# Hybrid decoder layer on one core: q, k and x transposed on TensorE in place of DMA transposes

## The chip, the cores and the metric

The kernel runs on one core of one Trainium2 chip. The metric is the device time of one execution in microseconds; the median of three runs counts. Engines are named as the profile names them: PE is TensorE, PEld its weight loads, DVE is VectorE, ACT is ScalarE, POOL is GpSimd, SP is the engine whose queue issues most DMAs.

## What is computed

One layer of a decoder (2048 positions, 1024 channels): an RMS norm, one input projection, three causal mixers side by side, and one output projection.

```
h = rms_norm(x, norm_g);  proj = h @ w_in
FoX (8 heads of 64):   softmax(q.k/8 + c[t] - c[s], s <= t) @ v,   q and k RMS-normed, c = cumsum(log_sigmoid(ff + b_f))
pooling (4 groups):    (trailing mean over 2/4/8/16 positions - the token) @ w_pool * scale
stick-breaking (4 heads): a = exp(log_sigmoid(z) + sum of -softplus(z) after s), s < t;  a @ v
out = x + concat(fox * silu(g), pool * silu(g), stick * silu(g)) @ w_out
```

Inputs and output are float32. The kernel keeps that precision by splitting each operand of a large matmul into a float16 high part and a float16 low part.

## The kernel before

**Stages.** Positions are cut into 16 blocks of 128 rows. Stage a is the projection and attention of FoX heads 0 to 3, stage b of heads 4 to 7, stage s of the four stick-breaking heads with the pooling projection (p) between its blocks, and stage o the output projection. In the profiled execution they lie roughly at 0 to 470, 470 to 820, 820 to 1235 and 1235 to 1416 us; they overlap at the edges. Sequence order is reversed, so block i attends to blocks 0 to i.

**A block's input.** `transpose_rows` (line 371) takes 128 rows of x, writes high and low parts side by side into a tile `pp` of 128x2048 f16 (`pairs16`, lines 341 and 342: one ACT cast, one DVE subtraction), and one DMA transpose turns it into `xT` (`xTx` in the trace), with channels on the partitions. `project` (line 315) then runs 24 matmuls of 128x512 per 512 output columns (`pqk`, `pvg`). Stage a makes x this way; the transposed x is also parked in DRAM (`keep_x`) and stages b, s and p load it from there (`xTb`, `xTs`, `xTp`). Stage o makes its own (`xTm` from `ppm`).

**q and k.** `stacks` (line 455) writes high and low parts of q and k of a block into `st` (128x1024 f16, by two calls of `pairs16`), and one DMA transpose on SP's queue turns it into `qT`. Five projection segments later `place` (line 466) runs on DVE: one copy puts k into the column block of `Kc` (line 467), two copies of 64x512 swap q's halves inside `qT` (line 469). Each of the 48 blocks of stages a, b and s does this once.

**Attention.** For each head `scores` (line 396) takes a PSUM tile `sp` of 128x1024 f32. The tag `sp` has two such tiles, two banks each. In stages a and b DVE reads it (line 736), in stage s ACT does (the sigmoid, line 875). ACT takes the exponential (line 746) or DVE scans (line 883), ACT or DVE casts the high part, POOL subtracts for the low part (`split_t`, lines 430 to 433), and a DMA transpose on SP's queue turns the weights into `tt` (line 435) for `pv`.

**What sets the order.** `projections` is a stream of segments of three matmuls (`SEG`: 16 per block), and the loop at the end advances it between heads by a table of goals (`LEADS`, `DEPTH`). `later(k, fn)` postpones work by k segments. From that program order a scheduler derives each engine's order; every engine then works its own list strictly from the front, with semaphores between them.

Of the kernel before, what the change touches and what calls it, by code (L numbers as in the profile page):

```python
# [10 lines left out]
F16 = mybir.dt.float16  # L11
# [7 lines left out]
P = 128  # L19
KT = 8  # L20
# [10 lines left out]
LB = 4  # L31
SPD = 6
KPD = 2
MXD = 0
GTD = 0
BAL = 1
GR4 = 0
GR2 = 1
QSB = 2
SWE = 'vv'  # L40
KCE = 'v'
SCD = 5
M5 = 2
FE = 's'
OMS = 'g'
# [72 lines left out]
KB = 5  # L118
QB = 1
QNB = 1  # L120
QTB = 3
WINDOWS = (2, 4, 8, 16)


# [1 line left out]
def hybrid(ctx: ExitStack, tc, xN, w_in, w_pT, w_out, ng, b_f, qg, kg, w_pool, p_scale, bands, out):  # L126
# [19 lines left out]
    def pick(pattern, k):  # L146
        return {"v": v, "g": g, "s": s}[pattern[k % len(pattern)]]
# [223 lines left out]
    def transpose_rows(src, scale, tag, park=None):  # L371
        pp = at.tile([P, 2 * D], F16, name=f"pp{tag}", tag="pp", bufs=PB)
        pairs16(pp[:, 0:D], pp[:, D:2 * D], src, scale[:, 0:1], pick(XLO, park or 0))
        x = xp.tile([P, 2, KT, P], F16, name=f"xT{tag}", tag="xT", bufs=XB)
        sy.dma_start_transpose(x.rearrange("p a k t -> p (a k) t"), pp)
        if park is not None:
            keep_x(park, x)
        return x

    def keep_x(j, x):  # L380
        later(KPD, lambda: dq(QPARK).dma_start(xTd[j], x))
# [68 lines left out]
    def heads(ap):  # L450
        return ap.rearrange("p (h d) -> p h d", h=NH)

    placed, spread_, mixed = set(), set(), set()

    def stacks(tag, j, qsrc, ksrc, sc, Kc):

        st = at.tile([P, 2, NH, P], F16, name=f"st{tag}", tag="qs", bufs=QSB)
        pairs16(st[:, 0, :, 0:HD], st[:, 0, :, HD:P], heads(ksrc), sc)
        pairs16(st[:, 1, :, 0:HD], st[:, 1, :, HD:P], heads(qsrc), sc)
        qT = at.tile([P, 2 * NH, P], F16, name=f"qT{tag}", tag="qT", bufs=QTB)  # L460
        if j % 4 == 3:
            Kc[j // 4] = big.tile([P, NH, 512], F16, name=f"K{tag}", tag="K", bufs=KB)
        o_ = (j % 4) * P
        sy.dma_start_transpose(qT, st.rearrange("p a h d -> p (a h d)"))

        def place():
            pick(KCE, 0).tensor_copy(Kc[j // 4][:, :, o_:o_ + P], qT[:, 0:NH])
            for k in range(2):
                pick(SWE, k).tensor_copy(qT[k * HD:k * HD + HD, 0:NH], qT[HD - k * HD:P - k * HD, NH:2 * NH])  # L469
            placed.add(tag)  # L470

        later(SCD, place)
        return qT

    def values(ph, i, j, Vc, src):
        if i % 4 == 0:
# [17 lines left out]
    class Fox:  # L494
        def __init__(self, ph, w, cols):
            self.ph, self.w, self.cols = ph, w, cols
            self.first = ph == "a"
            self.col = 0 if self.first else 256
            self.Vc = {}
            self.ctx = {}  # L500
            self.late = []

        def start(self):
# [200 lines left out]
        def stages(self, i, j, pqk):  # L704
            ph = self.ph
            qn = at.tile([P, 512], F32, name=f"qn{ph}_{i}", tag="qn", bufs=QNB)
            s.activation(qn, pqk, AF.Square)
            ss = sm.tile([P, 8], F32, name=f"ss{ph}_{i}", tag="ss")
            yield
            v.tensor_reduce(ss, qn.rearrange("p (h d) -> p h d", d=HD), AX.X, ALU.add)  # L710
            v.tensor_scalar(ss, ss, self.i2[:, 0:1], EPS, ALU.mult, ALU.add)
            f = sm.tile([P, 8], F32, name=f"f{ph}_{i}", tag="f")
            rsqrt(f, ss, 8, f"qk{ph}_{i}")
            yield
            v.tensor_scalar(f, f, self.iq[:, 0:1], None, ALU.mult, ALU.bypass)
            v.tensor_tensor(qn.rearrange("p (h d) -> p h d", d=HD), pqk.rearrange("p (h d) -> p h d", d=HD),
                            f.unsqueeze(2).broadcast_to([P, 2 * NH, HD]), ALU.mult)
            g.tensor_tensor(heads(qn[:, 256:512]), heads(qn[:, 256:512]), gain.unsqueeze(1).broadcast_to([P, NH, HD]), ALU.mult)
            yield
            self.ctx[i] = stacks(f"{ph}_{i}", j, qn[:, 0:256], qn[:, 256:512], 1.0, self.Kc)  # L720

        def qk(self, i, h):
            ph, negc = self.ph, self.negc
            j = NT - 1 - i
            qT = self.ctx[i]
            cs = list(chunks(j * P))
            n_ = len(cs)
# [59 lines left out]
    class Stick(Fox):  # L787
        def __init__(self, w):
            self.ph, self.w = "s", w
            self.Vc, self.ctx, self.late = {}, {}, []  # L790
            self.first = False
            self.col = 768
            self.vr, self.own = {}, {}
# [48 lines left out]
        def proj(self, i, x):  # L842
            w = self.w
            j = NT - 1 - i
            pqk = pj.tile([P, 512], F32, name=f"pqks_{i}", tag="pj")
            if i in IS:
                pvg = pj.tile([P, 512], F32, name=f"pvgs_{i}", tag="pj")
                yield from together([project(pqk, x, w, 0, 0, 512), project(pvg, x, w, 0, 512, 512)])
            else:
                yield from project(pqk, x, w, 0, 0, 512)  # L850
            qT = stacks(f"s_{i}", j, pqk[:, 0:256], pqk[:, 256:512], 1.0 / WS, self.Kc)
            if i not in IS:
                pvg = pj.tile([P, 512], F32, name=f"pvgs_{i}", tag="pj")
                yield from project(pvg, x, w, 0, 512, 512)
            vt = at.tile([P, NH, P], F16, name=f"vr_{i}", tag="fq", bufs=2)
            pairs16(vt[:, :, 0:HD], vt[:, :, HD:P], heads(pvg[:, 0:256]), 1.0 / WS)
            self.vr[i] = vt
            keep_gate("s", i, j, pvg[:, 256:512], w.iw, 768)
            self.steps(i, j)
            self.ctx[i] = qT  # L860

        def qk(self, i, h):
            j = NT - 1 - i
            qT = self.ctx[i]
            parts = []
            rprev = None
            if h == 0:
# [252 lines left out]
    def projections():  # L1120
        for u, (n, i) in enumerate(units):
            need_x(u + (2 if units[u + 2:u + 3] == [(4, 0)] and OA else LAH[n]))
            if i == 0 and n:
                phases[n].start()
            gen = phases[n].proj(i, xs.pop(u, None))
            yield from with_tail(gen) if (n, i) == (4, 0) else gen
            if i == NT - 1 and n < 3:
                with first(HLW):
                    load_weights((1, 2, 4)[n])
            if n == 2 and i == 1:  # L1130
                load_weights(3)
# [84 lines left out]
    with tc.manual_schedule(engines={mybir.EngineType.PE}) if MAN else nullcontext():  # L1216
        opening()
        for k, (n, i) in enumerate(plan):
# [2 lines left out]
            advance(base)  # L1221
            for h in range(NH):
                key = f"{ph.ph}_{i}"
                if key not in placed or ph.ph != "s" and key not in spread_:
                    tick(1 << 30)
                assert key in placed and (ph.ph == "s" or key in spread_)
                with first(HAT):
                    pending.append((ph, i, h, *ph.qk(i, h)))
                advance(base + (goal[k] - base) * (h + 1) // NH)
                drain(DEPTH)  # L1230
            ph.ctx.pop(i)
            if n == 1 and M5 <= i < M5 + 4:
                for kt in range(2 * (i - M5), 2 * (i - M5) + 2):
                    phases[3].fold(kt)
# [78 lines left out]
```

## Time and profile before

| | us |
|---|---|
| median of three runs (1412.66 to 1419.62) | 1414.28 |
| profiled execution | 1417.73 |
| its span, first to last instruction | 1415.7 |

| engine | busy share of the span |
|---|---|
| PE | 85% |
| DVE | 70% |
| ACT | 50% |
| POOL | 45% |
| 16 DMA engines, the SP/ACT queue with the transposes | 80.4% |

A busy share is a mean over four stages with different limits. PE's busy time counts from the start of a matmul to its modelled end, so two that overlap are not added. "issue" in a chain of waits is time in which an engine waited for nothing that the profile shows.

### The profile page before, as it was taken

The page shows a single profiled execution, that of the slowest core. Times are in us where ns is not written, and L with a number is a line of the kernel's source. Part 1 is how long each engine was busy: PE and PEld are TensorE (multiplying, and loading weights), DVE is VectorE, ACT ScalarE, POOL GpSimd, SP SyncE. Part 2 cuts the span into 40 slices and gives each one's busy share as a digit, 9 for nine tenths or more (in the row PEclk, how much of TensorE's full clock was granted, in tenths as well). Part 3 has the DMA queues.
Part 4 walks back from the last instruction along what each step waited for, and adds up shares of the span by engine and source line. Part 5 has one row for each costly group of instructions (what it writes and reads, how often), then busy time and mean ns, then how long its engine had stood idle before and what let it go on. Part 6 is the DMA issues. An engine that isn't in the chain of part 4 may idle for free.

```text
span 1415.7 us, 24981 instructions
## 1 busy us (share of the span) xinstructions
PE 1209.6 (85%) x9068; PEld 642.2 (45%) x9068; DVE 997.1 (70%) x2093; ACT 702.0 (50%) x1356; POOL 634.1 (45%) x615
## 2 busy tenths in 40 slices
PE   7788879787887889897987888978988997779998
PEld 3344445444444445454544544444544553444443
DVE  5777889889998567786888655556574669865731
ACT  6555546555554446664667644545455564432210
POOL 0133345445455234553656654555455464623300
PEclk9889899999998989999999999999999999989999
DMA  6689999998999999996999998687886888999853
GB/s 215 176 169 203 214 188 221 200 196 182 210 210 209 210 227 207 202 177 135 184 217 191 227 207 186 146 158 161 173 175 142 172 196 226 225 277 287 225 160 89
DMA packets 617068, 275.25 MB, mean 194 GB/s; under 512 B 552561, under 2 KB 590833, under 8 KB 616945
## 3 DMA queue, kind: packets, MB, share of 16 engines
q1 hardware_dynamic: 605600, 239.93, 80.4%
q10 hardware_dynamic: 10832, 33.67, 7.9%
q8 instruction: 71, 1.16, 0.4%
q14 instruction: 53, 0.43, 0.1%
q0 software_dynamic: 512, 0.07, 0.0%
HBM read 102.60 MB, written 34.67 MB: 97 GB/s over the span
## 4 chain that ended last, share of the span: by engine, by line
PE 18%; DVE 11%; issue 9%; DMA 8%; POOL 8%; ACT 5%; SPq 1%; POOLq 0%; ACTq 0%; DVEq 0%
PE pr L319 11%; DVE rrs L883 5%; POOL pps L433 5%; DMA qTs<-sts 2%; DMA qTb<-stb 2%; PE pqks L319 2%; DVE Lb L736 2%; DMA xTm<-ppm 1%; ACT pps L430 1%; ACT Lb L746 1%; POOL rrs L877 1%; PE sps L404 1%; DMA ttb<-ppb 1%; PE pp L319 1%; POOL ppb L433 1%
## 5 line engine op out<-in xcount | busy, mean ns | idle before, releaser
L433 POOL TENSOR_TENSOR ppb<-Lb,ppb 128x1024 f16<-128x1024 f32 (+7 forms) x96 | 151.6, 1593 | 150.3 <-ACT ppb L430 68.9
L433 POOL TENSOR_TENSOR ppa<-La,ppa 128x1024 f16<-128x1024 f32 (+7 forms) x96 | 152.7, 1604 | 141.9 <-DVE ppa L432 53.4
L433 POOL TENSOR_TENSOR pps<-rrs,pps 128x640 f16<-128x640 f32 (+7 forms) x96 | 171.3, 1790 | 75.2 <-ACT pps L430 74.8
L319 PE MATMUL pr<-wo,xTm 128*128 128x512 f16 x768 | 172.2, 386 | 8.1 <-DMA xTm<-ppm 5.3
L883 DVE TENSOR_TENSOR_SCAN rrs<-rrs 128x640 f32<-128x640 f32 (+7 forms) x64 | 109.5, 1714 | 68.3 <-POOL rrs L877 43.8
L430 ACT CAST pps<-rrs 128x640 f16<-128x640 f32 (+7 forms) x96 | 76.1, 796 | 142.0 <-DVE rrs L883 127.3
L746 ACT ACTIVATE Lb<-Lb,nmb 128x640 f32<-128x640 f32 (+7 forms) x96 | 85.6, 892 | 80.3 <-DVE nmb L740 75.4
L746 ACT ACTIVATE La<-La,nma 128x640 f32<-128x640 f32 (+7 forms) x96 | 85.5, 891 | 77.0 <-DVE nma L740 53.5
L319 PEld LDWEIGHTS <-xTm 128*128 128x128 f16 x768 | 75.8, 99 | 100.9 <-issue 8.8
L319 PEld LDWEIGHTS <-xTb 128*128 128x128 f16 x768 | 77.0, 103 | 92.6 <-issue 16.7
L404 PE MATMUL spa<-Ka,qTa 128*128 128x512 f16 (+3 forms) x320 | 83.7, 371 | 36.8 <-DVE mma L736 35.2
L319 PEld LDWEIGHTS <-xTs 128*128 128x128 f16 x768 | 74.4, 99 | 86.9 <-issue 3.3
L319 PEld LDWEIGHTS <-xTx 128*128 128x128 f16 x720 | 72.6, 105 | 89.3 <-issue 25.5
L319 PE MATMUL pqkb<-wb,xTb 128*128 128x512 f16 x384 | 101.7, 408 | 0.3 <-ACT wb L277 0.3
L404 PE MATMUL spb<-Kb,qTb 128*128 128x512 f16 (+3 forms) x320 | 79.7, 361 | 23.4 <-DVE mmb L736 20.7
L319 PE MATMUL pp<-auxp,xTp 128*128 128x512 f16 x384 | 96.9, 404 | 0.0
L319 PE MATMUL pqka<-wa,xTx 128*128 128x512 f16 x336 | 95.3, 434 | 1.3 <-DVE cr L562 1.3
L319 PE MATMUL pvgb<-wb,xTb 128*128 128x512 f16 x384 | 96.1, 390 | 0.0
L875 ACT ACTIVATE rrs<-sps,nc 128x640 f32<-128x640 f32 (+7 forms) x96 | 80.5, 863 | 30.3 <-PE sps L404 28.8
L319 PE MATMUL pqks<-ws,xTs 128*128 128x512 f16 x384 | 92.1, 385 | 0.7 <-DVE vo L342 0.4
L404 PE MATMUL sps<-Ks,qTs 128*128 128x512 f16 (+3 forms) x320 | 73.2, 361 | 21.2 <-DVE qTs L469 16.6
L319 PE MATMUL pvgs<-ws,xTs 128*128 128x512 f16 x384 | 90.9, 379 | 0.0
(307 smaller groups left out, 2804.4 us busy)
## 6 DMA issues: line engine op xcount, KB each, us to landing
xn<-in_xN_dram SPq DMA_DIRECT2D x16, 512.0 KB, 5.5
xTd<-xTx ACTq DMA_DIRECT2D x16, 512.0 KB, 4.3
xTb<-xTd ACTq DMA_DIRECT2D x16, 512.0 KB, 4.6
xTs<-xTd ACTq DMA_DIRECT2D x16, 512.0 KB, 4.3
xTp<-xTd ACTq DMA_DIRECT2D x16, 512.0 KB, 4.3
go<-gat SPq DMA_DIRECT2D x16, 512.0 KB, 7.6
mt<-mix SPq DMA_DIRECT2D x16, 512.0 KB, 5.6
xr<-in_xN_dram SPq DMA_DIRECT2D x16, 512.0 KB, 4.4
```

Of the source, the lines that this page charges most:

```text
L319: t.matmul(psum, x[:, xa, kt, :], wt[:, wa, c0:c0 + n], start=(kt == 0 and i == 0), stop=(kt == KT - 1 and i == 2))
L404: t.matmul(sp[:, b - c0 + off:e - c0 + off], qT[:, a * NH + h, :], Kc[b // 512][:, h, b % 512:b % 512 + e - b], start=(a == 0), stop=(a == ...
L430: s.copy(hi, p32)
L433: lo_eng.tensor_tensor(lo, p32, hi, ALU.subtract)
L736: v.tensor_tensor_reduce(lt, sp, negc[:, h, c0:c1_], c1[:, 0:1], 4 * NEG if a == 0 else mm[:, a - 1:a], ALU.add, ALU.max, mm[:, a:a + 1])
L746: s.activation(ls[a], ls[a], AF.Exp, bias=nm[:, 0:1], accum_out=la[:, a, h:h + 1])
L875: s.activation(gg, sp, AF.Sigmoid, scale=self.nc2[:, 0:1])
L877: g.affine_select(gg[:, 0:P], gg[:, 0:P], [[1, P]], ALU.is_gt, 1.0, base=0, channel_multiplier=-1)
L883: v.tensor_tensor_scan(gg, gg, gg, init, ALU.mult, ALU.bypass)
```

## The change

q and k are no longer transposed by a DMA. `stacks` only fills `st`; `place`, now a function of its own, is called when the attention of a block comes near: at the second, third or fourth head of the block before (the first of these at which `st` has been written by the program), or at the block's own first head if that has not happened. It takes one of the two `sp` tiles as `pt`, runs eight 128x128 transposes on PE, and five ACT copies out of PSUM: one of k into `Kc` (128x512), four of 64x512 that write q's high parts to both halves of `qT` and q's low parts likewise. DVE's three copies are gone. `st` has three buffers in place of two, `qT` two in place of three.

x's rows: where `park` is given (13 blocks at their turn and block 0 once more for the later stages, 14 in all; blocks 0 to 2 of the opening keep another path), the DMA transpose is replaced by `turn`, which is postponed by `TURN` = 11 projection segments after the split: sixteen 128x128 transposes into an `sp` tile and two ACT copies of 128x1024 into `xT`. The parking DMA follows as before. If `xT` is needed sooner, the list of postponed work is run at once. The transposes of the weights (`tt`) and of stage o (`xTm`) stay with the DMA.

```diff
+TURN = 11
-QSB = 2
-SWE = 'vv'
-KCE = 'v'
-SCD = 5
+QSB = 3
-QTB = 3
+QTB = 2
@@ transpose_rows
-        x = xp.tile([P, 2, KT, P], F16, name=f"xT{tag}", tag="xT", bufs=XB)
-        sy.dma_start_transpose(x.rearrange("p a k t -> p (a k) t"), pp)
-        if park is not None:
+        if park is None:
+            x = xp.tile([P, 2, KT, P], F16, name=f"xT{tag}", tag="xT", bufs=XB)
+            sy.dma_start_transpose(x.rearrange("p a k t -> p (a k) t"), pp)
+            return x
+        made_x = []
+
+        def turn():
+            x = xp.tile([P, 2, KT, P], F16, name=f"xT{tag}", tag="xT", bufs=XB)
+            pt = ps.tile([P, 2048], F16, name=f"pt{tag}", tag="sp")
+            for b in range(2 * KT):
+                t.transpose(pt[:, b * P:(b + 1) * P], pp[:, b * P:(b + 1) * P], idh)
+            for a in range(2):
+                s.copy(x[:, a], pt[:, a * D:(a + 1) * D].rearrange("p (k t) -> p k t", k=KT))
+            made_x.append(x)
             keep_x(park, x)
-        return x
+
+        later(TURN, turn)
+        return made_x
@@ stacks, place
-        qT = at.tile([P, 2 * NH, P], F16, name=f"qT{tag}", tag="qT", bufs=QTB)
-        sy.dma_start_transpose(qT, st.rearrange("p a h d -> p (a h d)"))
-
-        def place():
-            pick(KCE, 0).tensor_copy(Kc[j // 4][:, :, o_:o_ + P], qT[:, 0:NH])
+    def place(tag):
+        st, kc = stacked.pop(tag)
+        qT = at.tile([P, 2 * NH, P], F16, name=f"qT{tag}", tag="qT", bufs=QTB)
+        pt = ps.tile([P, 2048], F16, name=f"pt{tag}", tag="sp")
+        for a in range(2):
+            for h in range(NH):
+                b = (a * NH + h) * P
+                t.transpose(pt[:, b:b + P], st[:, a, h, :], idh)
+        k_, q_ = (pt[:, a * 512:(a + 1) * 512].rearrange("p (h b) -> p h b", h=NH) for a in range(2))
+        s.copy(kc, k_)
+        for a in range(2):
             for k in range(2):
-                pick(SWE, k).tensor_copy(qT[k * HD:k * HD + HD, 0:NH], qT[HD - k * HD:P - k * HD, NH:2 * NH])
-            placed.add(tag)
-
-        later(SCD, place)
-        return qT
+                s.copy(qT[k * HD:(k + 1) * HD, a * NH:(a + 1) * NH], q_[a * HD:(a + 1) * HD])
+        placed[tag] = qT
@@ the loop over blocks and heads
+                if key not in placed:
+                    place(key)
+                elif h and k + 1 < len(plan):
+                    up = f"{phases[plan[k + 1][0]].ph}_{plan[k + 1][1]}"
+                    if up in stacked:
+                        place(up)
```

How the instructions then stand is seen at three places. The names carry stage, block, head and chunk: `rrs_10_2_0` is the weights' tile of stage s, block 10, head 2, chunk 0.

DVE in stage s, where block 11's q and k become ready during block 10, before:

```order
L883 SCALAR_TENSOR_TENSOR rrs_10_1_1_12493<-rrs_10_1_1_12493,rrs_10_1_0_12478 128x512
L342 SCALAR_TENSOR_TENSOR sts_11_12515<-pqks_11_12430,sts_11_12515 128x4x64 x2
L467 COPY Ks_8_11547<-qTs_11_12520 128x4x128
L469 COPY qTs_11_12520<-qTs_11_12520 64x512 x2
L883 SCALAR_TENSOR_TENSOR rrs_10_2_0_12576<-rrs_10_2_0_12576 128x896
```

and of the change:

```order
L899 SCALAR_TENSOR_TENSOR rrs_10_1_1_13177<-rrs_10_1_1_13177,rrs_10_1_0_13162 128x512
L342 SCALAR_TENSOR_TENSOR sts_11_13199<-pqks_11_13114,sts_11_13199 128x4x64 x2
L342 SCALAR_TENSOR_TENSOR vr_11_13304<-pvgs_11_13204,vr_11_13304 128x4x64
L899 SCALAR_TENSOR_TENSOR rrs_10_2_0_13270<-rrs_10_2_0_13270 128x896
L926 SCALAR_TENSOR_TENSOR oms_9_13371<-os_9_13012,io_9688,oms_9_13371 128x256
```

The three copies that followed the low parts of block 11's q and k at once, and stood ahead of the scan of head 2, are gone from DVE.

ACT at the same place (line 875, in the change 891, is the sigmoid that frees a score tile), before:

```order
L341 ACTIVATE sts_11_12515<-pqks_11_12430 128x4x64
L430 CAST pps_10_1_1_12497<-rrs_10_1_1_12493 128x512
L341 ACTIVATE sts_11_12515<-pqks_11_12430 128x4x64
L875 ACTIVATE rrs_10_2_0_12576<-sps_10_2_0_12571,nc2_9124 128x896
L875 ACTIVATE rrs_10_2_1_12591<-sps_10_2_1_12588,nc2_9124 128x512
```

and of the change:

```order
L341 ACTIVATE sts_11_13199<-pqks_11_13114 128x4x64
L443 CAST pps_10_1_1_13181<-rrs_10_1_1_13177 128x512
L341 ACTIVATE sts_11_13199<-pqks_11_13114 128x4x64
L487 COPY Ks_8_12200<-pts_11_13251 128x4x128
L490 COPY qTs_11_13250<-pts_11_13251 64x512 x4
L891 ACTIVATE rrs_10_2_0_13270<-sps_10_2_0_13265,nc2_9686 128x896
```

Five copies now stand between block 11's casts and the sigmoid of head 2. On PE the eight transposes stand directly ahead of the scores `sps_10_2_0`.

PE in stage a, where x of block 7 (`xTx8`) is first used by `pf7`, before:

```order
L446 MATMUL oa_4_1_1804<-Va_0_504,tta_4_1_0_1559 128x128
...
L404 MATMUL spa_5_2_0_1919<-Ka_0_501,qTa_5_1472 128x512
...
L328 MATMUL pf7_1863<-wa_0_1_326,xTx8_1590 128x16
...
L329 MATMUL pf7_1863<-wa_0_1_326,xTx8_1590 128x8
```

and of the change:

```order
L384 MATMUL ptx8_1898<-idh_157,ppx8_1739 128x128
L577 MATMUL pf6_1743<-ident_146,cn6_1863 8x128
...
L459 MATMUL oa_4_1_1969<-Va_4_1431,tta_4_1_0_1711 128x128
...
L485 MATMUL pta_6_1982<-idh_157,sta_6_1882 128x128
...
L328 MATMUL pf7_2041<-wa_0_1_328,xTx8_1897 128x16
L319 LDWEIGHTS xTx8_1897
L319 MATMUL pqka_7_2040<-wa_0_325,xTx8_1897 128x512
...
L417 MATMUL spa_5_1_0_1997<-Ka_4_1313,qTa_5_1683 128x256
...
L329 MATMUL pf7_2041<-wa_0_1_328,xTx8_1897 128x8
```

The last of the sixteen transposes of x now stands one small transpose, ten matmuls of `pv` and block 6's eight transposes ahead of `pf7`, and the attention has come less far by then: of block 5 the scores of head 0 precede `pf7`, where those of heads 0 to 2 did.

## Rows read from the trace of the kernel before

**Rows 1.** The page: busy us, share, instructions by engine; the SP/ACT DMA queue.

```profile
PE 1209.6 (85%) x9068; PEld 642.2 (45%) x9068; DVE 997.1 (70%) x2093; ACT 702.0 (50%) x1356; POOL 634.1 (45%) x615
...
q1 hardware_dynamic: 605600, 239.93, 80.4%
```

**Rows 2.** Busy time by stage (a, b, s): columns as in the first line.

```profile
core 0: us, PE busy (x) PEld busy (x) DVE busy (x) ACT busy (x) POOL busy (x), PEclk, DMA share, GB/s
60.00:470.00 410.00, 339.58 (x2598) 185.06 (x2599) 347.34 (x932) 222.57 (x511) 191.97 (x155) 0.91 0.97 198
470.00:820.00 350.00, 300.03 (x2239) 164.05 (x2238) 252.85 (x582) 201.96 (x418) 176.21 (x148) 0.95 0.98 198
820.00:1235.00 415.00, 356.38 (x3109) 191.88 (x3108) 265.37 (x313) 209.92 (x321) 223.38 (x279) 0.94 0.82 181
```

**Rows 3.** Chain that ended last, shares by line: 470 to 820, then 820 to 1235.

```profile
by line: issue 11.6%; DMA qTb<-stb 7.2%; DVE Lb L736 6.6%; ACT Lb L746 4.0%; DMA ttb<-ppb 3.3%; POOL ppb L433 3.0%; ACT ppb L430 2.7%; PE pvgb L319 2.6%; PE spb L404 2.5%; SPq L435 1.7%; DMA xTs<-xTd 1.5%; PE pqkb L319 1.5%; DVE stb L342 1.
...
by line: issue 22.1%; DVE rrs L883 15.6%; POOL pps L433 15.4%; DMA qTs<-sts 6.7%; PE pqks L319 5.5%; ACT pps L430 3.6%; POOL rrs L877 2.8%; PE pp L319 2.6%; PE sps L404 2.5%; DMA mt<-mix 2.2%; ACT rrs L875 2.1%; PE pvgs L319 1.6%; DVE qTs L
```

**Rows 4.** The same chain in order of time, stage s: start us, us, what.

```profile
981.25 3.21 DMA qTs<-sts
984.48 0.31 DVE Ks L467
984.81 0.29 DVE qTs L469
...
985.43 1.77 DVE rrs L883
```

**Rows 5.** Who waited for whom, whole span: us in total, times, longest us.

```profile
PE spa L404 <- DVE mma L736: 35.2, 20, 4.9
...
DVE Ks L467 <- DMA qTs<-sts: 35.5, 12, 5.4
...
DVE Kb L467 <- DMA qTb<-stb: 23.5, 12, 5.9
...
PE spb L404 <- DVE mmb L736: 20.7, 13, 4.1
...
PE ob L446 <- DMA ttb<-ppb: 20.6, 16, 3.9
...
PE sps L404 <- DVE qTs L469: 16.6, 5, 7.1
...
DVE Ka L467 <- DMA qTa<-sta: 13.9, 8, 3.0
...
PE pf L328 <- DMA xTx<-ppx: 11.0, 7, 2.8
```

**Rows 6.** Small matmuls on PE: two in order of time; transposes of f32 in the opening.

```profile
517.95 0.22 PE L446 MATMUL ob<-Vb,ttb 128*128 128x128 f16 x1
518.01 0.19 PE L447 MATMUL ob<-Vb,ttb 128*128 128x64 f16 x1
...
L571 PE MATMUL xt<-ident,xn x8: 421/421/447, 4.7 to 6.2; 128*128 128x128 f32 x8
```

**Rows 7.** ACT out of PSUM, by shape: busy us, mean ns, idle before.

```profile
L707 ACT ACTIVATE qnb<-pqkb 128x512 f32<-128x512 f32 x16 | 9.4, 586 | 11.4 <-PE pqkb L319 8.0 <-DVE stb L342 3.4
...
L875 ACT ACTIVATE rrs<-sps,nc 128x1024 f32<-128x1024 f32 x28 | 30.9, 1113 | 7.6 <-PE sps L404 7.4
```

**Rows 8.** DVE busy us of line 469, then of line 467, over the whole span.

```profile
0.00:1416.00 1416.00, 51.07 (x96) 0.94 0.89 194
...
0.00:1416.00 1416.00, 26.30 (x48) 0.94 0.89 194
```

**Rows 9.** SP issuing the transposes that go: ns min/median/max.

```profile
L464 SPq DMA_TRANSPOSE qTs<-sts x16: 1232/1554/3673, 756.6 to 1173.0; - x16
...
L375 SPq DMA_TRANSPOSE xTx<-ppx x16: 1317/1936/6172, 19.3 to 337.9; - x16
```

More of the change, by code (lines that the diff above doesn't have):

```diff
@@ L186, in hybrid @@
     g.tensor_copy(id16, ident)
+    idh = const.tile([P, P], F16, name="idh")
+    g.tensor_copy(idh, ident)
     zero = at.tile([P, P], BF16, name="zero", tag="oa")
@@ L451, in heads @@
         return ap.rearrange("p (h d) -> p h d", h=NH)
-    placed, spread_, mixed = set(), set(), set()
+    stacked, placed, spread_, mixed = {}, {}, set(), set()
     def stacks(tag, j, qsrc, ksrc, sc, Kc):
@@ L459, in stacks @@
         pairs16(st[:, 1, :, 0:HD], st[:, 1, :, HD:P], heads(qsrc), sc)
-        qT = at.tile([P, 2 * NH, P], F16, name=f"qT{tag}", tag="qT", bufs=QTB)
         if j % 4 == 3:
             Kc[j // 4] = big.tile([P, NH, 512], F16, name=f"K{tag}", tag="K", bufs=KB)
-        o_ = (j % 4) * P
-        sy.dma_start_transpose(qT, st.rearrange("p a h d -> p (a h d)"))
-        def place():
-            pick(KCE, 0).tensor_copy(Kc[j // 4][:, :, o_:o_ + P], qT[:, 0:NH])
+        stacked[tag] = (st, Kc[j // 4][:, :, j % 4 * P:(j % 4 + 1) * P])
+    def place(tag):
[9 more added lines that the diff above has]
+        for a in range(2):
             for k in range(2):
-                pick(SWE, k).tensor_copy(qT[k * HD:k * HD + HD, 0:NH], qT[HD - k * HD:P - k * HD, NH:2 * NH])
-            placed.add(tag)
-        later(SCD, place)
-        return qT
+                s.copy(qT[k * HD:(k + 1) * HD, a * NH:(a + 1) * NH], q_[a * HD:(a + 1) * HD])
+        placed[tag] = qT
     def values(ph, i, j, Vc, src):
@@ L499, in __init__ @@
             self.Vc = {}
-            self.ctx = {}
             self.late = []
@@ L719, in stages @@
             yield
-            self.ctx[i] = stacks(f"{ph}_{i}", j, qn[:, 0:256], qn[:, 256:512], 1.0, self.Kc)
+            stacks(f"{ph}_{i}", j, qn[:, 0:256], qn[:, 256:512], 1.0, self.Kc)
         def qk(self, i, h):
@@ L724, in qk @@
             j = NT - 1 - i
-            qT = self.ctx[i]
+            qT = placed[f"{self.ph}_{i}"]
             cs = list(chunks(j * P))
@@ L789, in __init__ @@
             self.ph, self.w = "s", w
-            self.Vc, self.ctx, self.late = {}, {}, []
+            self.Vc, self.late = {}, []
             self.first = False
@@ L850, in proj @@
                 yield from project(pqk, x, w, 0, 0, 512)
-            qT = stacks(f"s_{i}", j, pqk[:, 0:256], pqk[:, 256:512], 1.0 / WS, self.Kc)
+            stacks(f"s_{i}", j, pqk[:, 0:256], pqk[:, 256:512], 1.0 / WS, self.Kc)
             if i not in IS:
@@ L859, in proj @@
             self.steps(i, j)
-            self.ctx[i] = qT
         def qk(self, i, h):
             j = NT - 1 - i
-            qT = self.ctx[i]
+            qT = placed[f"{self.ph}_{i}"]
             parts = []
@@ L1124, in projections @@
                 phases[n].start()
-            gen = phases[n].proj(i, xs.pop(u, None))
+            x = xs.pop(u, None)
+            if isinstance(x, list):
+                if not x:
+                    tick(1 << 30)
+                x = x[0]
+            gen = phases[n].proj(i, x)
             yield from with_tail(gen) if (n, i) == (4, 0) else gen
@@ L1223, in hybrid @@
                 key = f"{ph.ph}_{i}"
-                if key not in placed or ph.ph != "s" and key not in spread_:
+                if ph.ph != "s" and key not in spread_:
                     tick(1 << 30)
-                assert key in placed and (ph.ph == "s" or key in spread_)
+                assert ph.ph == "s" or key in spread_
+                if key not in placed:
[4 more added lines that the diff above has]
+                        place(up)
                 with first(HAT):
@@ L1230, in hybrid @@
                 drain(DEPTH)
-            ph.ctx.pop(i)
+            placed.pop(key)
             if n == 1 and M5 <= i < M5 + 4:
```

## The prediction

> **What bounds the kernel now.** I read the page first for the busy shares, then the same by stage, then the chain of waits of the two stages that it covers, and last the list of who waited for whom. The page shows no engine at its limit: PE 85%, DVE 70%, ACT 50%, and the DMA queue that carries the transposes 80.4% [rows 1]. By stage the picture is closer: in stage a DVE is busy for 347 of 410 us and PE for 340, in b and s PE for 300 of 350 and 356 of 415; the DMA share is 0.97, 0.98 and 0.82 [rows 2]. So several resources are near their limit together, and the end is set by what they wait for in turn. The chain says so: in stage b its largest single line, apart from issue, is the DMA of q and k, 7.2% of 350 = 25.2 us; in stage s it is 6.7% of 415 = 27.8 us, behind the scan and POOL's subtraction [rows 3]. One such place in time: the DMA takes 3.21 us, DVE's copies of line 467 and 469 come at once, and only behind them the next scan [rows 4]. DVE works strictly in order, so a copy that waits for a DMA holds back score reads and scans that have nothing to do with it. DVE stood for 35.5 + 23.5 + 13.9 = 72.9 us like this [rows 5]. PE in turn waited 35.2 + 20.7 us for DVE to read a score tile, 16.6 us for the swap of q's halves, 11.0 us for x and 20.6 us for transposed weights in stage b [rows 5].
>
> **The basis.** The sum is made on the profiled execution, 1417.7 us (span 1415.7 and 2.0 around it). The median is 3.5 us lower, which I take off at the end.
>
> **Removed: the wait for q and k.** On the chain it is 25.2 + 27.8 = 53.0 us in b and s, against 59.0 us of DVE standing in the two [rows 3, 5]. The chain does not reach stage a; at the same ratio DVE's 13.9 us there are 12.5. The upper end is thus 65.5 us; the lower is nothing, if another wait is just as late. I take a's 12.5 whole, since DVE is 85% busy there [rows 2] and is the pace, and half of b's and s's, 26.5, because behind the DMA the chain goes on over ACT, POOL and "issue" [rows 3], and these are late next: **-39 us**.
>
> **Removed: DVE's copies.** Lines 467 and 469 are 26.3 + 51.1 = 77.4 us of DVE [rows 8]. How much of a DVE microsecond lies on the path I read from the chain over the busy time: in b (6.6 + 1.5)% of 350 is 28.4 us of 252.9 busy, 0.11; in s 15.6% of 415 is 64.7 of 265.4, 0.24 [rows 2, 3]. At the mean of 0.18: **-14 us** (bounds 9 and 19).
>
> **Removed: 62 DMA transposes** (48 of q and k, 14 of x). They free SP for 48 x 1.55 + 14 x 1.94 = 102 us of issuing [rows 9], and 48 x 0.262 + 14 x 0.524 = 19.9 MB of the queue's 239.93 MB [rows 1], 8%. The weights' transposes stand behind them on the same queue; PE waited 20.6 us for those of stage b [rows 5]. Between nothing and that I take a third: **-7 us**.
>
> **Moved: x's transposes in stage a.** PE waited 11.0 us for the DMA of x [rows 5]. Now x's first use stands close behind its sixteen transposes; ACT must copy 128x1024 twice, at 1.11 us each by the nearest row out of PSUM [rows 7]. The first copy can run beside the second eight transposes, and `pv` and block 6's transposes cover about a microsecond, so about one copy is bare: 14 x 1.11 = 16 us at most, none at best. Less the 11.0 that go, the bounds are -11 and +5; I take **0**. The parking DMA follows the copy; its reader comes a stage later, which hides it. If ACT is late at that place, PE stands with all that is queued behind `pf`, projection and attention alike.
>
> **Added on PE: 48 x 8 + 14 x 16 = 608 transposes.** No row shows one of 16-bit data. The nearest is a 128x128 f16 matmul of `pv` with its own weight load: the next matmul starts 0.06 us later [rows 6], 36 us in all. The other bound is the opening's transposes of f32, eight within 1.5 us from first to last start, 0.214 us apart [rows 6], 130 us in all. I take the first, whose data has the same width. On the path: the chain has (2.6 + 2.5 + 1.5)% of 350 = 23 of 300 us of PE in b and (5.5 + 2.6 + 2.5 + 1.6)% of 415 = 51 of 356 in s, 0.08 and 0.14 [rows 2, 3]; 36 x 0.11: **+4 us**. The upper bound is dealt with as a rival.
>
> The Trainium skill (TensorE: Matmul & The Clock Gate, Part 4: PE-mode transpose) speaks against the cheap price: it gives about 275 ns for such a transpose inside a kernel, and says that transposes do not count as activity for the clock. By that price 608 of them are 167 us, an estimate from that page. The trace's f32 transposes last 421 ns each but start every 214 ns [rows 6]: what lasts and what holds the engine differ there by a factor of two.
>
> **Added on ACT: 48 x 5 + 14 x 2 copies.** By the nearest rows, 586 ns for 512 columns and 1113 ns for 1024 out of PSUM [rows 7], 240 x 0.586 + 28 x 1.113 = 172 us; a copy of 64 partitions is priced like one of 128. ACT rises from 702 to some 874 us, 62% of the span. On the path: in b (4.0 + 2.7)% of 350 = 23.5 of 202 us, in s (3.6 + 2.1)% of 415 = 23.7 of 210, 0.115 in both [rows 2, 3]: **+20 us**. Queued behind the copies on ACT are a sigmoid or an exponential, for which DVE and POOL wait. If ACT's idle time is no cover, the cost is up to 172 us; if it always is, nothing.
>
> **Added: 62 users of the two score tiles.** Each `pt` takes one of two tiles from its first transpose to ACT's last copy. PE waited 35.2 + 20.7 = 56 us for score tiles in a and b [rows 5], over 2 x 96 tiles, 0.29 us each, and next to nothing over the 96 of s; over all 288 that is 0.19. At that rate 62 more cost **+12 us**; the bounds are 0 and one whole read by ACT each, 62 x 1.11 = 69 us [rows 7].
>
> **Sum:** -39 - 14 - 7 + 0 + 4 + 20 + 12 = -24. 1417.7 - 24 = 1393.7 for a profiled execution, less 3.5: **1390 us**, 1.7% faster.
>
> **The rivals.**
> *The DMA wait sets the pace alone.* All 65.5 us of it come off, and half of what is added hides: -65.5 - 14 - 7 + 2 + 10 + 6 = -69, 1345 us. For it: in b and s the DMA is on the chain nearly block by block. Against it: ACT, POOL and DVE each hold other pieces of the chain [rows 3].
> *The work only changes engine.* Softmax runs DVE, ACT, POOL in turn; DVE loses 77 us and ACT gains 172, so the same chain is as long as before and only a quarter of the wait, 16 us, is won: -16 - 14 - 7 + 4 + 20 + 12 = -1, 1413 us. For it: ACT is already 58% busy in b [rows 2] and stands in its chain.
> *The two score tiles become the bound, slower.* While a `pt` waits for ACT, the scores have one tile and no overlap of filling and reading. Place: PE ahead of the scores that follow a `pt`. Price: 69 us in place of 12, -24 + 57 = +33, 1447 us. It outweighs the gain from 12 + 24 = 36 us on, 0.58 us of PE standing per `pt`. For it: PE already waits for these tiles [rows 5]. Against it: DVE reads them sooner once it no longer waits for DMAs.
> *A transpose holds PE as long as one of f32.* 130 us in place of 36, all on the path, give 1390 + 94 = 1484 us. Against it: the narrow matmuls of [rows 6] start every 0.06 us. The page named above would have it dearer still.
> That the change does not do what it says is excluded by the order on the engines: the three copies are gone from DVE and the transposes stand on PE.
>
> **How the numbers follow.** Forecast 0.49, DMA wait alone 0.15, change of engine 0.20, score tiles 0.13, dear transposes 0.03. A measurement here can tell about 0.5% from no change, so "same" is 1407 to 1421. Faster: nearly all of the first (0.46), the second, and a little of the third (0.03): 0.64. Same: 0.03 + 0.13 of the third: 0.16. Slower: the last two and 0.04 of the third: 0.20. The range is 1350 to 1430: below it lies half of the DMA case (0.07), above it most of the tile case (0.10) and the dear transposes (0.03).
>
> **What would show it.** Right: no wait of DVE for q or k; the start of one transpose to the next near 0.06 us; DVE's busy time down by about 77 us and ACT's up by 140 to 200; PE's wait for x's copy near a microsecond per block in stage a; PE's waits for score tiles not above some 70 us in total; stages a, b and s each shorter by 5 to 15 us and stage o unchanged. Wrong: PE waits of a microsecond or more behind most `pt` tiles; ACT with the copies as a main part of the chain; transposes 0.2 us apart; or a stage a that is longer because attention stands further behind the projection, as its order shows.

## The result, and the profile after

The change made the kernel slower: 1436.8 us (four runs, 1430.1 to 1437.6) against 1416.9 (1412.7 to 1421.0) of the kernel before, a ratio of 1.013 [1.008, 1.018]. The prediction was 1390, with a range that ended at 1430, and "faster" at 0.64. The sign was wrong, and the time lies 7 us outside the range.

The profiled execution has a span of 1434.8 us. Its page:

```profile
PE 1236.9 (86%) x9676; PEld 677.6 (47%) x9676; DVE 931.4 (65%) x1949; ACT 858.2 (60%) x1623; POOL 649.9 (45%) x616
...
q1 hardware_dynamic: 525792, 220.00, 71.1%
...
PE 23%; ACT 11%; DVE 9%; issue 9%; POOL 8%; DMA 5%; SPq 1%; ACTq 0%; POOLq 0%; DVEq 0%
```

Against [rows 1], DVE lost 66 us, ACT gained 156, and the transposes' queue went from 80.4% to 71.1%. Forecast were some 77 less for DVE and 140 to 200 more for ACT. In the chain of waits over the whole span (last line) ACT holds 11%, where it had 5% before:

```profile
PE 18%; DVE 11%; issue 9%; DMA 8%; POOL 8%; ACT 5%; SPq 1%; POOLq 0%; ACTq 0%; DVEq 0%
```

Where the time is, stages tell. [Rows 2] cut the span at fixed times; below it is cut at the first projection matmul of each stage (`pqka`, `pqkb`, `pqks`, `pr`), so that the same work is compared. First before, then after; stages a, b, s, o:

```profile
core 0: us, PE busy (x) PEld busy (x) DVE busy (x) ACT busy (x) POOL busy (x), PEclk, DMA share, GB/s
44.20:374.60 330.40, 271.26 (x2010) 145.92 (x2007) 273.89 (x805) 180.22 (x429) 141.03 (x120) 0.90 0.94 198
374.60:726.10 351.50, 302.05 (x2228) 164.13 (x2227) 267.68 (x624) 190.41 (x412) 166.63 (x127) 0.93 0.96 197
726.10:1214.50 488.40, 417.87 (x3628) 227.52 (x3627) 315.52 (x425) 262.93 (x424) 272.70 (x329) 0.95 0.87 184
1214.50:1415.70 201.20, 184.92 (x1070) 87.63 (x1069) 112.36 (x156) 39.52 (x38) 51.11 (x26) 0.96 0.77 210
```

```profile
45.40:391.60 346.20, 283.82 (x2335) 165.73 (x2332) 251.01 (x754) 242.18 (x524) 139.50 (x116) 0.91 0.71 156
391.60:741.30 349.70, 303.10 (x2360) 170.00 (x2360) 241.40 (x574) 231.50 (x485) 170.35 (x129) 0.95 0.86 182
741.30:1235.40 494.10, 434.04 (x3815) 239.13 (x3814) 304.31 (x384) 316.04 (x522) 285.41 (x329) 0.95 0.81 177
1235.40:1434.80 199.40, 182.08 (x1026) 85.40 (x1022) 106.96 (x154) 39.14 (x37) 51.73 (x26) 0.96 0.79 210
```

Stage a lost 15.8 us, b won 1.8, s lost 5.7, o won 1.8; the opening lost 1.2. Nearly the whole loss is stage a. There PE is busy for 12.6 us more than before and stands without work for 62.4 us after 59.1: the waits that went came back at other places.

What PE and DVE waited for, whole span (us in total, times, longest), answering [rows 5]:

```profile
DVE Lb L753 <- PE spb L417: 31.7, 19, 5.0
...
DVE La L753 <- PE spa L417: 28.8, 19, 4.9
...
PE ob L459 <- DMA ttb<-ppb: 22.8, 19, 3.3
...
PE spa L417 <- DVE mma L753: 16.0, 13, 3.3
...
PE spb L417 <- DVE mmb L753: 12.1, 12, 2.7
...
ACT Ks L487 <- PE pts L485: 11.6, 7, 3.6
...
PE pts L485 <- DVE sts L342: 9.1, 6, 5.5
...
PE ptx L384 <- ACT ppx L341: 7.3, 3, 5.0
...
PE pta L485 <- DVE sta L342: 6.9, 3, 3.6
...
PE ptx L384 <- DVE ppx L342: 6.1, 6, 1.4
```

The first two lines as they stood before:

```profile
DVE Lb L736 <- PE spb L404: 5.5, 8, 1.0
...
DVE La L736 <- PE spa L404: 3.2, 3, 2.1
```

No wait of DVE for q or k is left. In its place DVE waits for scores: 28.8 and 31.7 us in a and b, where it was 3.2 and 5.5. PE, which owes those scores, waits less for free score tiles in a and b than before (16.0 + 12.1 against 35.2 + 20.7), but it now stands ahead of transposes, mostly for the low and high parts that DVE and ACT have not written yet.

The longer of the two waits for `sta` in stage a, in order of time: block 6's q and k during block 5's attention (start us, us, what, idle before):

```profile
250.40 1.03 PE L384 MATMUL ptx<-idh,ppx 128*128 128x128 f16 x8 [1.36 <-DVE ppx L342]
...
251.90 3.08 DVE L342 SCALAR_TENSOR_TENSOR sta<-qna,sta 128x256 f16<-128x256 f32 x2
...
255.04 1.03 PE L485 MATMUL pta<-idh,sta 128*128 128x128 f16 x8 [3.61 <-DVE sta L342]
...
256.11 0.59 ACT L487 COPY Ka<-pta 128x512 f16<-128x512 f16 x1 [2.30 <-PE pta L485]
...
256.60 2.35 ACT L490 COPY qTa<-pta 64x512 f16<-64x512 f16 x4
...
258.14 0.63 PE L417 MATMUL spa<-Ka,qTa 128*128 128x256 f16 x2
...
259.88 1.02 DVE L753 CUSTOM_DVE_ANT_0 La<-spa,negca,c 128x768 f32<-128x768 f32 x1 [4.89 <-PE spa L417]
```

PE has nothing to do for 3.6 us because its next instruction is a transpose of parts that DVE is still writing. Behind it in PE's list, after a few matmuls of the projection and of `pv`, stand the next scores (`spa`), for which DVE then stands 4.9 us (last line). ACT in turn stands 2.3 us for the transposes. The work that PE does so early is wanted only a block later.

### The profile page after: what moved, and what is told of

Its sections match the earlier page's. It is cut to its first block, busy times and chain, and to the rows that moved or that the text cites. A ratio compares the mean times of both kernels' runs of the same rounds, so it can differ in the third digit from the quotient of the medians.

```text
span 1434.8 us, 26212 instructions
## 1 busy us (share of the span) xinstructions
PE 1236.9 (86%) x9676; PEld 677.6 (47%) x9676; DVE 931.4 (65%) x1949; ACT 858.2 (60%) x1623; POOL 649.9 (45%) x616
## 3 DMA queue, kind: packets, MB, share of 16 engines
q1 hardware_dynamic: 525792, 220.00, 71.1%
## 4 chain that ended last, share of the span: by engine, by line
PE 23%; ACT 11%; DVE 9%; issue 9%; POOL 8%; DMA 5%; SPq 1%; ACTq 0%; POOLq 0%; DVEq 0%
PE pr L319 10%; POOL pps L446 4%; DVE rrs L899 4%; DMA ttb<-ppb 3%; DVE Lb L753 2%; ACT Lb L763 2%; PE pp L319 2%; PE pqks L319 2%; PE pqkb L319 2%; PE pvgs L319 1%; PE sps L417 1%; ACT ppb L443 1%; ACT pps L443 1%; ACT qTb L490 1%; ACT qTs L490 1%
## 5 line engine op out<-in xcount | busy, mean ns | idle before, releaser
L446 POOL TENSOR_TENSOR pps<-rrs,pps 128x640 f16<-128x640 f32 (+7 forms) x96 | 174.8, 1828 | 69.1 <-ACT pps L443 69.1
L319 PE MATMUL pr<-wo,xTm 128*128 128x512 f16 x768 | 171.3, 385 | 10.6 <-DVE ym L1021 5.7
L899 DVE TENSOR_TENSOR_SCAN rrs<-rrs 128x640 f32<-128x640 f32 (+7 forms) x64 | 106.5, 1667 | 70.9 <-POOL rrs L893 47.1
L319 PEld LDWEIGHTS <-xTb 128*128 128x128 f16 x768 | 73.8, 100 | 86.6 <-issue 12.1
L319 PEld LDWEIGHTS <-xTx 128*128 128x128 f16 x720 | 68.1, 100 | 72.9 <-issue 4.4
L319 PE MATMUL pqkb<-wb,xTb 128*128 128x512 f16 x384 | 96.1, 395 | 3.4 <-DVE wb L278 1.8
L319 PE MATMUL pqks<-ws,xTs 128*128 128x512 f16 x384 | 96.4, 395 | 2.3 <-ACT ws L277 1.3
L319 PE MATMUL pp<-auxp,xTp 128*128 128x512 f16 x384 | 91.7, 389 | 3.5 <-DVE vo L342 2.4
L319 PE MATMUL pvgb<-wb,xTb 128*128 128x512 f16 x384 | 92.9, 383 | 0.0
L417 PE MATMUL sps<-Ks,qTs 128*128 128x512 f16 (+3 forms) x320 | 78.2, 370 | 16.5 <-ACT rrs L891 9.8
L417 PE MATMUL spb<-Kb,qTb 128*128 128x512 f16 (+3 forms) x320 | 78.6, 358 | 13.4 <-DVE mmb L753 12.1
L319 PE MATMUL pqka<-wa,xTx 128*128 128x512 f16 x336 | 83.8, 391 | 0.0
```

Source lines behind the costliest of these rows:

```text
L319: t.matmul(psum, x[:, xa, kt, :], wt[:, wa, c0:c0 + n], start=(kt == 0 and i == 0), stop=(kt == KT - 1 and i == 2))
L417: t.matmul(sp[:, b - c0 + off:e - c0 + off], qT[:, a * NH + h, :], Kc[b // 512][:, h, b % 512:b % 512 + e - b], start=(a == 0), stop=(a == ...
L446: lo_eng.tensor_tensor(lo, p32, hi, ALU.subtract)
L899: v.tensor_tensor_scan(gg, gg, gg, init, ALU.mult, ALU.bypass)
```

## The experiments

The theory (D in the expectations, reached after `x_only`, `qk_only`, `pt_pj` and `dup_q`): it is the place of the transposes in PE's order. Issued from the second head of the block before, they stand ahead of scores that are wanted now, while their own inputs are not ready. The rivals: x's transposes (A); the work itself, ACT's copies or the transposes, wherever they stand (B); the two score tiles that `pt` takes (C); and chance, since every other place draws another order from the scheduler (F). All ratios are to the kernel before, run beside each.

**x alone, and q and k alone.** `x_only` leaves q and k to the DMA, with the buffers of before; `qk_only` leaves x to it. In the diffs `QKT` names the stages whose q and k go to PE, and `XT` = 0 is the DMA for x.

```diff
# x_only
-QKT = 'abs'
-QSB = 3
-QTB = 2
+QKT = ''
+QSB = 2
+QTB = 3
# qk_only
-XT = 1
+XT = 0
```

> Only x goes through TensorE (224 transposes, 14 tiles of two ACT copies); q and k keep DMA transpose and DVE copies, with the buffer counts of before. Theory A: all the loss and none of the gain, 1432 to 1445 us. Theory B: 224 x 0.056 = 13 us more work, about the wait for x's DMA saved, 1418 to 1425. Theory C: 14 of 62 tiles, 1418 to 1421.

> Only q and k go through TensorE (384 transposes, 48 tiles); x keeps its DMA transpose, the rest as in the change. Theory A, x's turn in stage a is the loss (PE stands ahead of its transposes for the split, then for the copy): this kernel is faster than before, 1400 to 1408 us, with stage a no longer than before. Theory B, PE's own added work counts whole in every stage: 22 us of transposes less some 15 of waits, about 1422. Theory C, the extra users of the two score tiles: 48 of 62 remain, about 1430.

`x_only` took 1408.5 us, 0.994 [0.991, 0.997]; `qk_only` 1449.9, 1.023 [1.017, 1.029]. Both lie outside what A, B and C expected: x is a small gain, and q and k are the loss. Stage a of `x_only`:

```profile
43.80:362.30 318.50, 275.85 (x2219) 155.91 (x2215) 257.80 (x801) 201.03 (x451) 141.87 (x118) 0.94 0.84 183
```

It is 11.9 us shorter than before.

**The score tiles.** `pt_pj` is the change with every `pt` in the pool of the projections' PSUM tiles; `qk_pj` is the same without x.

```diff
-        pt = ps.tile([P, 2048], F16, name=f"pt{tag}", tag="sp")
+        pt = pj.tile([P, D], F16, name=f"pt{tag}", tag="pj")
```

> The change with its transposes in PSUM tiles of the projection's pool (one bank for q and k, two single banks for x), so that the two score tiles are left to the scores. Theory C: most of the loss comes back, 1400 to 1415 us. Theories A and B: as the change, 1430 to 1440; above that if the projection's four banks become short.

> Only q and k through TensorE, as in qk_only (1449.9 us, 1.023 of before), with the PSUM tile of the transposes in the projection's pool instead of one of the two score tiles. Theory C (score tiles): the ratio falls by 1.2 to 2.3 points, to 1.000 to 1.011. Theory D (PE stands ahead of the transposes for DVE's low parts of q and k, and ACT's five copies come late): 1.015 to 1.025.

`pt_pj` took 1419.7 us, 1.002 [1.000, 1.004]; `qk_pj` 1414.8, 0.997 [0.995, 0.999]. At the place of the change the other pool takes 1.1 points off, and 2.6 without x. That spoke for the tiles, until the place itself was moved.

**The place.** In the change the next block's transposes may go from the second head on (`h` = 1). `look2` and `look3` wait for the third and the fourth, `own` for the first head of the block itself.

```diff
-                elif h and k + 1 < len(plan):
+                elif h >= 3 and k + 1 < len(plan):
```

> The change with the transposes of the next block's q and k allowed only at the last head of the block before, not from its second head on. Theory D: PE no longer stands for the low parts, ratio 1.000 to 1.006. Theory C: as many tiles are taken from the scores, ratio 1.010 to 1.018; more if the copies now come too late for the block's first scores.

> The change with the next block's q and k allowed from the third head on (the change: second, 1.013; look3: fourth, 0.984; own: the block's own first, 1.040). Theory D (transposes whose low parts are late hold back the scores behind them): between the two, 0.990 to 1.005. Theory F (a chance of the order that the scheduler makes): anywhere from 0.98 to 1.03, not between.

> The change with q and k transposed only at the block's own first head (look3, ratio 0.984, does it at the last head of the block before). Theory D (what counts is that no score of the current block stands behind transposes whose input is late): as look3, 0.980 to 0.988. Theory E (there is a best distance: the five ACT copies now stand between the transposes and the block's first scores, 2.9 us bare per block): 48 x 1 to 3 us more, 1.01 to 1.08.

`look3` took 1394.2 us, 0.984 [0.980, 0.988]; `look2` 1392.5, 0.983 [0.981, 0.985]; `own` 1474.5, 1.040 [1.036, 1.043]. D had the direction of the first two but not the size, and it had `own` wrong. The same instructions on the same engines, with the same tiles, go from 1.3% slower to 1.6 or 1.7% faster than before when one number is changed. `look3` by stage (a, b, s, o, as above):

```profile
43.70:351.90 308.20, 273.36 (x2319) 158.77 (x2316) 241.94 (x744) 233.16 (x513) 134.54 (x116) 0.95 0.77 170
351.90:701.20 349.30, 304.68 (x2375) 171.40 (x2372) 243.92 (x583) 239.45 (x497) 177.28 (x130) 0.94 0.91 189
701.20:1193.50 492.30, 433.80 (x3822) 239.26 (x3821) 295.20 (x386) 315.84 (x522) 277.57 (x329) 0.95 0.81 176
1193.50:1390.50 197.00, 180.60 (x1029) 84.77 (x1025) 106.40 (x154) 39.26 (x38) 51.99 (x26) 0.96 0.80 212
```

Of the 44.3 us between its profiled span and the change's, 38.0 are stage a's (346.2 to 308.2). Its waits (here scores are line 443, q's and k's transposes 528):

```profile
DVE Lb L797 <- PE spb L443: 36.7, 28, 6.0
...
DVE La L797 <- PE spa L443: 8.7, 8, 2.6
PE pts L528 <- DVE sts L354: 8.1, 4, 4.0
...
PE ptx L410 <- ACT ppx L353: 2.9, 2, 2.6
...
PE ptx L410 <- DVE ppx L354: 2.7, 3, 1.6
```

In stage a DVE waits 8.7 us for scores in place of 28.8, PE 5.6 us for x's parts in place of 13.4, and PE's wait for `sta`, 6.9 us in the change, is gone. Where little was won over the change, in b and s, the waits stayed (36.7 and 8.1 against 31.7 and 9.1). `look2` wins its 43.3 us in other parts, 23.2 in a and 11.5 in b, where DVE's wait for scores is down to 21.4 us. Its stages a and b, and that wait:

```profile
43.80:366.80 323.00, 278.69 (x2332) 162.02 (x2328) 250.08 (x760) 242.48 (x528) 137.73 (x116) 0.94 0.76 168
366.80:705.00 338.20, 297.54 (x2362) 168.15 (x2362) 235.00 (x573) 235.40 (x489) 173.91 (x129) 0.97 0.90 191
...
DVE Lb L797 <- PE spb L443: 21.4, 22, 2.8
```

In stage a, PE's idle time just before the transposes of q, k and x goes roughly along with the length of the stage, whichever edit took it away (one trace of each):

| kernel | PE idle just before these transposes, us | stage a, us |
|---|---|---|
| `qk_only` | 20.9 | 350.6 |
| the change | 25.4 | 346.2 |
| `qk_pj` | 15.6 | 339.7 |
| `pt_pj` | 13.2 | 331.0 |
| `look2` | 6.5 | 323.0 |
| `look3` | 5.6 | 308.2 |

That is 19.8 of the 27.5 us of idle time between the change and `look3` in stage a. It does not hold in stage s, where `look3` stands longer at `pts` than the change (19.2 us and 14.0). The granted clock in stage a is 0.95 against 0.91. If a mean of 0.91 is a mix of 1.2 and 2.4 GHz, 18% of 346.2 us, 62 us, were spent at the lower level, and 10% of 308.2, 31 us, in `look3`; at half the clock those 31 us more do the work of some 15, so by this estimate the clock alone is a good part of the 38. The rows do not show what part of it came first; the kernel before had 0.90 there, so the clock does not explain why the change is slower than that.

`own` is too late. Its waits:

```profile
PE spa L443 <- ACT qTa L385: 15.0, 10, 3.1
...
PE sps L443 <- ACT qTs L385: 5.7, 4, 2.9
...
PE spb L443 <- ACT qTb L385: 3.7, 5, 1.4
```

With the transposes directly ahead of the block's first scores, PE stands for ACT's copies, 24.4 us in all, as E expected. That is under half of what `own` loses; the rest was not followed up.

**Place and tile together.** `look3_pj` is `look3` with q's and k's `pt` in the projections' pool (x's keeps a score tile); `qk_look3` is `look3` without x.

> look3 with the tile of q's and k's transposes in the projection's pool. Theory C (the score tile costs by itself): another 1 to 2 points, ratio 0.965 to 0.978. Theory D (the tile mattered because it tied the scores' order to late transposes): within 0.6 points of look3, 0.978 to 0.990, and stage s nearer qk_pj's 481 us.

> qk_only (ratio 1.023) with look3's place for the transposes, x by DMA as before. Theory D: the place alone is worth as much without x's turn, 2 to 3 points: 0.992 to 1.003, and PE's excess ahead of pta in stage a falls from 23 us to under 3. Theory C: the tiles are still taken, 1.010 to 1.025.

`look3_pj` took 1411.0 us, 0.997 [0.995, 1.000]: at the better place the other pool costs 1.3 points, which neither C nor D expected. So a score tile is not dear in itself: it costs time at the early place and saves some at the late one. And the place matters with the score tiles: with them the two places lie 2.9 points apart, with the other pool 0.5 (`pt_pj` 1.002, `look3_pj` 0.997, which differ in x's tiles too). The loss needs both. Why the other pool costs time here was not tested (the attention's outputs share it). `qk_look3` took 1401.1 us, 0.988 [0.984, 0.991], where `qk_only` had 1.023: the place turns q and k from a loss of 2.3% into a gain of 1.2%. Three pairs of kernels, each apart by the place alone, gain 2.9 points or more, which makes chance (F) unlikely; no run draws another order at the same place.

**What a microsecond of the added work costs.** `dup_q` does each of the 384 transposes of q and k twice, `dup_c` each of the five copies twice, `look3_dupc` the latter in `look3`.

```diff
# dup_q: around the transposes in place; dup_c, look3_dupc: around the copies
+        for _ in range(2):
```

> The change with each of the 384 transposes of q and k done twice into the same place (nothing else is added). Theory B: 384 x 0.056 = 21 us at full clock more, 1455 to 1462 us. Theories A and C: PE's idle time takes most of it, at most 7 us more, 1436 to 1444.

> The change with each of the five ACT copies per block of q and k done twice: 48 x 5 x 0.58 = 139 us more of ACT, and the score tile held 2.9 us longer per block. Theory C with ACT as what holds the tile: 40 us or more above the change, ratio over 1.04. Prediction's price of ACT alone (0.115 of it on the path): 16 us, ratio 1.024. ACT's idle time covers it: ratio under 1.018.

> look3 with q's and k's five ACT copies done twice, 139 us more of ACT. Theory D with ACT's price as on the change (0.66 of it): 92 us more, ratio 1.045 to 1.055. If in look3 the copies lie beside other work: 16 us or less, ratio under 0.996.

`dup_q` took 1447.7 us, 1.021 [1.019, 1.023], 0.8 points or 11 us over the change, for 384 transposes at 0.056 us = 21.5 us: about half of it reaches the end, though by the two intervals it may be a fifth or four fifths. `dup_c` took 1529.0 us, 1.079 [1.075, 1.083], and ACT was busy for 993.2 us:

```profile
PE 1265.9 (83%) x9676; PEld 688.4 (45%) x9676; DVE 913.4 (60%) x1949; ACT 993.2 (65%) x1865; POOL 634.2 (42%) x616
```

135 us more of ACT are 6.6 points, 93 us: 0.69. `look3_dupc` took 1484.5, 1.046 [1.039, 1.052]: 6.1 points, 87 us for 134 of ACT (991.2 less 856.8): 0.65. The prediction's share was 0.115. The doubled copies also hold the score tile and q's tile longer, so this is the price of ACT's time at this spot and not of any microsecond of ACT.

**Fewer copies.** `copy2` transposes q's halves in pieces of 64 columns, so that both copies of each come out of PE in place; two ACT copies remain of five, and PE has 20 transposes per block in place of 8.

```diff
+                for k in range(2):
+                    t.transpose(pt[k * HD:(k + 1) * HD, b:b + P], st[:, 1, h, a * HD:(a + 1) * HD], idh)
+        s.copy(kc, pt[:, 0:512].rearrange("p (h b) -> p h b", h=NH))
+        s.copy(qT, pt[:, 512:1536].rearrange("p (h b) -> p h b", h=2 * NH))
```

> The change with two ACT copies per block of q and k instead of five (128x512 and 128x1024, some 1.6 us instead of 2.9) and with twenty transposes instead of eight (sixteen of 64 columns write q's halves twice): 48 x 1.3 = 62 us less of ACT, 576 more transposes on PE. If ACT costs as dup_c showed (92 us for 139) and PE as dup_q (11 us for 384 transposes): -41 + 16, ratio 0.990 to 1.000. If dup_c's price holds only for more load: -7 + 16, ratio 1.015 to 1.025.

> look3 with the two ACT copies of copy2. If ACT's time still counts there: ratio 0.968 to 0.980. If look3 has taken the copies off the path: PE's 16 us remain, ratio 0.984 to 0.996.

`copy2` took 1418.0 us, 1.001 [0.998, 1.004]; ACT is busy for 794.9 us. 63 us of ACT less, and 576 transposes more, are together worth 1.2 points, 17 us: 0.26 per microsecond of ACT if the transposes are free. If each costs what `dup_q` showed, half of 0.056 us, they take 16 us (an estimate), and ACT's microsecond is worth (17 + 16) / 63 = 0.5. `look3_copy2` took 1386.3, 0.977 [0.972, 0.982], the fastest of all: 0.7 points below `look3`, though the two intervals touch; it lies where it was expected if ACT's time still counts at the better place. Whether copies taken away are worth less per microsecond than copies added, these runs do not settle.

**Stage b alone.** Stage b became 1.8 us shorter in the change. `mix_b` is `x_only`, with its counts of buffers, and q and k on PE in stage b only, at the change's place.

```diff
-QKT = ''
+QKT = 'b'
```

> x through TensorE as in x_only (ratio 0.994), q and k through TensorE in stage b alone, by DMA in a and s. If stage b's shorter time in the change and in qk_only (2 and 10 us) is a gain of its own: 2 to 10 us below x_only, ratio 0.987 to 0.993. If stage b only won back what stage a had left undone: 0 to 8 us above x_only, ratio 0.994 to 1.000.

`mix_b` took 1423.1 us, 1.003 [1.000, 1.007], against 0.994 of `x_only`, above what either reading expected. Stage b's 1.8 us were no gain that could be had this way: it took 354.4 us (353.8 in `x_only`), and most of the loss lies in stage s (502.5 after 491.2), whose q and k go by DMA in both. Why stage s loses there stays open.

## Why the prediction was wrong

The sum came to -24 us; the change did +18 (1.3% of 1417). By its steps:

- **The place of the transposes had no term.** This is the step that failed. The sum priced what the transposes and copies take, and the tiles they use, but not where PE meets them; a `pt` had the same price wherever it stood. Moving q's and k's one or two heads later is worth 2.9 to 3.0 points, about 42 us, which is the whole gap. In stage a, PE stood 25.4 us just before transposes, so the waits that were to be won were spent again; with the score tile taken meanwhile, DVE stood 28.8 us for scores in place of 3.2. The prediction had both halves of it: the order showed block 6's eight transposes ahead of `pf7` and of block 5's scores, and its last part named a longer stage a as a sign of error; yet DVE, which writes `sta`, was read as "85% busy" and not as late for PE. What would have shown it is when the low parts of the block ahead are finished, against when PE comes to that point of its list.
- **Wait for q and k, -39.** The wait went, as predicted. But b and s, which were to give 26 of the 39, gave 1.8 and -5.7 in the end, with all that was added there; in `look3` 2.2 and -3.9, in `look2` 13.3 and -1.6. DVE's wait for a DMA became a wait of DVE for scores and of ACT for the transposes (11.6 us ahead of `Ks`, 10.6 of `Kb`, 4.0 of `Ka`). In `look3` the gain is stage a's: 22 us, where 12.5 stood in the sum.
- **DVE's copies, -14; the queue, -7.** DVE's 66 us (of 77) and the queue's 9 points are there; no run shows alone what either was worth. PE's wait for stage b's transposed weights, on which the second term rested, is 22.8 us after 20.6 [rows 5], so nothing shows that the freed queue helped.
- **x, 0.** `x_only` at 0.994, some 8 us, is inside its bounds; stage a alone is 11.9 us shorter, at their edge.
- **PE's transposes, +4.** Eight of `ptx` whose inputs were ready took 0.62 us with a last one of some 0.24, so they start 0.055 us apart, and 0.06 was right; at the lower clock (granted 0.52 at 250.3 us) eight took 1.03 us. The share of 0.11 was low: doubling them gave about 0.5, with a wide interval. The rival of dear transposes falls. The Trainium skill (TensorE: Matmul & The Clock Gate, Part 4: PE-mode transpose) gives about 275 ns for one in a kernel; here one lasts 225 to 253 ns on the mean, but PE starts the next long before. The same section of the Trainium skill has it that transposes do not count for the clock; stages b and s kept 0.95 and 0.95 with 128 of them in each, after 0.93 and 0.95, and stage a 0.91 after 0.90, so no loss against the kernel before shows.

```profile
248.43 0.62 PE L384 MATMUL ptx<-idh,ppx 128*128 128x128 f16 x8 [0.44 <-ACT ppx L341]
...
L384 PE MATMUL ptx<-idh,ppx 128*128 128x128 f16 x224 | 18.6, 236 | 16.9 <-ACT ppx L341 7.3 <-DVE ppx L342 6.1 <-DVE mma L753 3.5
L485 PE MATMUL pta<-idh,sta 128*128 128x128 f16 x128 | 12.3, 253 | 11.3 <-DVE sta L342 6.9 <-DVE nma L757 2.8 <-DVE mma L753 1.7
L485 PE MATMUL pts<-idh,sts 128*128 128x128 f16 x128 | 11.8, 230 | 14.0 <-DVE sts L342 9.1 <-ACT rrs L891 4.9
L485 PE MATMUL ptb<-idh,stb 128*128 128x128 f16 x128 | 10.5, 225 | 1.9 <-DVE mma L753 1.9
```

- **ACT's copies, +20.** Their time was right, 166 us for 172 (three groups of 37.1, 26.8, three of 9.3). The share was not: 0.115 was the chain's share over the busy share, and the runs have 0.26 to 0.5 for taking copies away at this place and 0.69 for adding some. At 0.26 the term is 43 us, and more at the others.
- **Score tiles, +12.** The scores' waits for tiles fell by half in a and b; the transposes' own (for `mma` and `rrs` in the lines above) are 12.0 us. The rival that had them turn the change slower named the right place, PE ahead of the scores behind a `pt`, and its 1447 us is the nearest of all; but its mechanism, PE standing for a tile that ACT holds, is a small part of what the waits show, and `look2` and `look3` are fast with the same tiles. Still the tile has its part: at the change's place the other pool is worth 1.1 points, 16 us, with x and 2.6 without.

That `look3` comes out at the forecast's ratio (0.984, and 1390 over 1414 is 0.983) is chance in part: its gain lies in stage a, x included, and not in b and s, where most of the forecast's lay; and ACT's copies cost more than the forecast had them at.

What stays open: how much of what `look3` wins over the change in stage a is PE standing and how much the clock that rose with it; and why `look2` wins in b what `look3` wins in a, and neither wins in s, where PE stands ahead of the transposes in all three.

## What to carry to other kernels

On an engine that works its list in order, work for the next block needs a place as well as a price: look for the point from which its inputs are surely written, and what stands behind it until then; too early stalls the present block, the more so if the early work holds a tile that the block needs, and too late leaves the evacuation bare (here 1.013, 0.983 and 1.040 for the same instructions). The share of a chain of waits says who held the path once, not what one more microsecond costs; doubling the work comes nearer to that (0.115 read, 0.65 to 0.69 measured). Where a change brings two moves, run each alone: one of these was a gain at once.

## What the runs showed of the hardware

ACT takes as long to copy 64 partitions as 128, by the rows of the change; what nearly halves the time is half the columns.

```profile
L490 ACT COPY qTa<-pta 64x512 f16<-64x512 f16 x64 | 37.1, 580 | 0.6
L386 ACT COPY xTx<-ptx 128x1024 f16<-128x1024 f16 x28 | 26.8, 1011 | 7.1 <-PE ptx L384 7.1
L487 ACT COPY Ka<-pta 128x512 f16<-128x512 f16 x16 | 9.3, 582 | 4.1 <-PE pta L485 4.0
```
